# Four unused tiles in layer 1: split weights, quarter sums and the last projection's tiles begin at other addresses modulo 256 bytes

## The chip, the core and the metric

The kernel runs on one core of a Trainium2 chip. The metric is the device time of one execution in microseconds (us). Addresses in this text are byte addresses inside one partition of the on-chip memory, as the built program assigns them; "modulo 256" is what is left of them after division by 256.

## The reference

Two layers of a diffusion backbone over 1024 latent and 256 context tokens of width 1024, all in float32. Layer 0 has neighbourhood attention and bidirectional mLSTM heads; layer 1, which the change touches, has 16 bidirectional HGRN2 heads:

```python
def _c_mixer(h_lat, h_ctx, w_in, lb, h_norm, w_out, need_ctx):
    def project(h):
        q, f_fwd, f_bwd, i, z = _split_cols(h @ w_in, C_SIZES)     # 5 x 2048 columns, 16 heads of 128
        ...
        rec = (_bht(_heads(jax.nn.silu(q), HG_HEADS)), _bht(_heads(i, HG_HEADS)), (decay(f_fwd), decay(f_bwd)))
        return rec, z
    ...
    o_l, o_c = _gla_bidir(rec_l, rec_c, need_ctx)                  # chunked scan, both directions

    def merge(o, z):
        o = _rms(jnp.swapaxes(o, 1, 2).astype(z.dtype), h_norm.reshape(HG_HEADS, HG_VDIM))
        return (o.reshape(o.shape[:2] + (HG_VW,)) * jax.nn.silu(z)) @ w_out
    return merge(o_l, z_l), ...
...
x = x + gate * y_lat
```

## The kernel before, in words

Every large product is made of three float32r matmuls. Each operand is split into a high part (rounded to float32r by ScalarE, ACT) and a low part (the rest, subtracted by VectorE, DVE). `dense` (L129 to L133) walks over the 128-row blocks k and issues high x high (L131), high x low (L132) and low x high (L133) into one accumulator. In the profile a matmul is named `out<-moving,stationary`: `mm<-wzh,hh` streams the weight tile wzh past the stationary block of hh. TensorE (PE) loads the stationary block of the next matmul (PEld) while the present one streams.

The activations after norm and modulation lie in `hh` and `hl` (128 partitions x 8 blocks x 1280 tokens). Layer 1 then has three stages.

- **Wide stage** (1832 to 2165 us of the profiled span). `hg_wide` computes queries and forget gates with a Strassen-like scheme on quarters. `half_sums` makes three sums of quarters of the activations in tiles st1h to st3l (st4 is a fourth, elsewhere). Matmuls `x<-st1h,wh`, `mm<-hh,wh` and so on stream 512 columns of a sum or of hh past a weight block of the ring w.
- **Head stage** (2165 to 3141 us), 16 heads of about 62.5 us. `hg_vt` and `hg_vz` project values and z with the split weights wzh and wzl. For 256 context tokens hh streams past wz (`mm<-hh,wzh`); for the latent tokens wz streams past hh (`mm<-wzh,hh`, 256 columns), eight runs of 24 matmuls in each head. `hg_intra` puts such a run between the seven levels of the recurrence, whose small matmuls (L1401, `s<-gQ,gksel`) wait for DVE's updates of gK and gQ (L1431) and ACT's copy gksel (L1436). After the levels come the state products (`s<-gv,gkn`), the scan (`s<-gS,gQ`, `s<-gv,gA`) and ACT's squares of its results (L1506).
- **Last projection** (3141 to 3317 us), again with a Strassen-like scheme: `c<-woh,yh`, `tr<-woh,yh` stream 512 columns of a split weight past a split block of the head outputs. Weights come from rings in the pools oy, w1 and wo1, the y blocks from oy and op1.

Pools are stacked, so a tile's address follows from what was allocated ahead of it. The order of instructions is set by a scheduler that works with modelled times and with the waits that reused memory brings: hga, hgb and hg (head stage) lie where st and s1 (wide stage) lay, and a tile there waits for the old tiles that it overlaps.

Addresses modulo 256 before: hh and hl 192; wzh and wzl 0; st1h to st3l 0, st4h and st4l 192; the weight ring w of layer 1 192; in the last projection y blocks 192 (oy) and 64 (op1), weights 192 (oy, w1) and 64 (wo1). In layer 0 hh is at 192 too, and the ring w at 128. "Distance" below means address of the moving tile minus address of the stationary one, modulo 256. Offsets inside these tiles are multiples of 256 bytes.

Of the kernel before, what the change touches and what calls it, by code (L numbers as in the profile page):

```python
# [10 lines left out]
F32 = mybir.dt.float32  # L11
# [8 lines left out]
P = 128  # L20
# [25 lines left out]
class Prog:  # L46
# [489 lines left out]
    def ml_load(self, h, pool):  # L536
        nc = self.nc
        st = {"k": {}, "q": {}, "v": {}, "S": {}}

        def load(t0, order):  # L540
            q = self.rope("q", h, t0, pool, "mqT", 6)
            kT = self.rope("k", h, t0, pool, "mkT", 2)
            for i in order:
# [15 lines left out]
                for j in range(2):  # L559
                    nc.tensor.matmul(ps, lhsT=kT[:, j, s], rhs=q[:, j, s], start=(j == 0), stop=(j == 1))  # L560
                st["S"][tt] = self.t(pool, [P, P], F32, "mST", MLB)
                nc.scalar.copy(st["S"][tt], ps)

# [24 lines left out]
    def ml_rec(self, h, st, pool, nxt):  # L588
# [20 lines left out]
        for i in range(NT):  # L609
            for d in range(2):  # L610
# [8 lines left out]
                nc.vector.scalar_tensor_tensor(  # L619
                    out=SD, in0=st["S"][c], scalar=KS, in1=Dm, op0=ALU.mult, op1=ALU.mult  # L620
                )
# [408 lines left out]
    def half_sums(self, pool, s1, tp, x):  # L1030
        A, chain = self.half_part, self.half_chain
        home = {1: s1, 2: pool, 3: pool, 4: tp}
        two = lambda n: [self.t(home[n], [P, 4, 512], F32R, f"st{n}{c}", 1) for c in "hl"]
        S = {n: two(n) for n in (2, 3, 1)}
        self.p1 = lambda u: self.t(tp, [P, 512], F32, "p1", 3)
        self.co = lambda: self.t(tp, [P, 512], F32, "co", 2)
        add, sub = ALU.add, ALU.subtract

        def done(n, j, y):
            self.split(S[n][0][:, j, :], S[n][1][:, j, :], y)  # L1040

        yield two(4)
        S[4] = two(4)
        x = x + [self.half_base(self.t(tp, [P, 512], F32, f"u{j}", 1), j) for j in (2, 3)]
        for j in range(4):
            done(1, j, x[j])
        yield
        for j in (2, 3, 0, 1):
            (h, l), (h2, l2) = A(0, 0, j), A(1, 0, j)
            y = self.co()  # L1050
            chain(y, h, (l, add))
            chain(x[j], x[j], (y, sub))
            done(2, j, x[j])
            chain(y, y, (h2, sub), (l2, sub))
            done(3, j, y)
        for j in (2, 3, 0, 1):
            h, l = A(0, 1, j)
            chain(x[j], h, (x[j], sub), (l, add))
            done(4, j, x[j])
        yield S  # L1060
# [506 lines left out]
    def build(self):  # L1567
        tc, nc, a = self.tc, self.nc, self.a
        dma = nc.sync.dma_start
        with ExitStack() as es:  # L1570
# [280 lines left out]
            with l1:  # L1851
                lo = ExitStack()
                sp, s1 = [lo.enter_context(tc.tile_pool(name=n, bufs=1, reuse_waits="tile")) for n in ("st", "s1")]
                pools = []

                def early():
                    lo.close()
                    for n, tags in (
                        ("hga", (("gq", 2, 512), ("gK", 1, 2 * LAT), ("gQ", 1, 2 * LAT), ("gkn", 4, 512), ("gksel", 1, LAT))),
                        ("hgb", ()),  # L1860
                    ):
                        pools.append(l1.enter_context(tc.tile_pool(name=n, bufs=2, reuse_waits="tile")))
                        for t, b, f in tags:
                            for _ in range(b):
                                self.t(pools[-1], [P, f], F32, t, b)
                    pools.append(self.wblock(
                        pools[1], "wz", [a["wc"][:, i * 2048 : i * 2048 + P] for i in (3, 4)], KD, 256, [tp, 7, "br"]
                    ))
                    pools.append(self.hg_proj(0, pools[0], FF)[0])

                with tc.tile_pool(name="sx", bufs=1, side="right", reuse_waits="tile") as tp, self.pp.phase(x=4):
                    self.hg_wide(sp, s1, tp, x, FF[2][0], early)
                    wf = self.wblock(
                        self.wp, "w", [a["wc"][:, 4096 + P : 4096 + 2 * P]], KD, P, [tp, 7, "br"], ring=self.slabs
                    )
                pool, wzp, wv, st = pools
                pool = _Two(
                    pool, wzp, l1.enter_context(tc.tile_pool(name="hg", bufs=2, reuse_waits="tile")),
                    ("gq", "gK", "gQ", "gkn", "gksel"), ("wzl", "wzh"),
                )  # L1880
# [124 lines left out]
                for t in range(4):  # L2005
# [3 lines left out]
                        1, False, True,  # L2009
                    )  # L2010
            with tc.tile_pool(name="op1", bufs=2) as op, ExitStack() as wl, tc.issue_after(w5_dma.ins):
                wl1 = wl.enter_context(tc.tile_pool(name="wo1", bufs=1))
                r16 += [(wl1, "wo", 12)] * 8
                w6 = block(self.sw[2], r16, later)
# [254 lines left out]
```

## Time and profile before

| | |
|---|---|
| runs | 3320.68, 3319.92, 3318.21 us; median 3319.92 |
| profiled execution | 3318.67 us, span from first to last instruction 3316.9 us |
| granted TensorE clock | 1.00 |
| PE busy | 3268.9 us (99%) |
| PEld busy | 2905.1 us (88%) |
| DVE, ACT, POOL busy | 2173.8 (66%), 1455.9 (44%), 796.5 us (24%) |
| mean DMA rate | 115 GB/s |

"Busy" of PE is the union of the matmuls' modelled spans, which overlap: a 128x256 matmul is shown for some 280 ns, while the next one starts some 115 ns after it. How fast PE goes is therefore read from the spacing of starts, not from the share of busy time or from a matmul's own duration.

### The profile page before, as it was taken

To read this page: it belongs to the slowest core of one execution; us is meant where nothing else is said; L and a number is where in the kernel's file an instruction comes from. 1 tells how busy PE (TensorE), PEld (TensorE's weight loads), DVE (VectorE), ACT (ScalarE), POOL (GpSimd) and SP (SyncE) were. 2 spreads that over 40 slices of the span, in tenths; PEclk is the share of its full clock that TensorE was granted. 3 is DMA by queue.
4 is the path that set the end of the run, shared out by engine and by line. 5 is a ranking of instruction groups with operands and counts; after the bars stand their busy time and mean duration, and the time that the engine had idled before them with its cause. 6 is when DMAs were issued, how large, how long until landed. Compare 5 with 4: busy or idle time off the path is not lost.

```text
span 3316.9 us, 64819 instructions
## 1 busy us (share of the span) xinstructions
PE 3268.9 (99%) x24814; PEld 2905.1 (88%) x24814; DVE 2173.8 (66%) x4978; ACT 1455.9 (44%) x3396; POOL 796.5 (24%) x1191
## 2 busy tenths in 40 slices
PE   7999999999999999999999999999999999999999
PEld 6699899988989888898888788899999999999977
DVE  5337666666655566687767755577677677677756
ACT  5335554455544444455446333333433433433443
POOL 2222222222211112221110233312333333333110
PEclk9999999999999999999999999999999999999999
DMA  7713222232233433444653333322322324334376
GB/s 246 247 52 84 85 71 82 69 94 84 72 87 105 145 113 123 131 141 144 210 179 100 100 102 105 104 74 76 120 76 93 117 79 112 95 85 107 91 213 165
DMA packets 338102, 379.82 MB, mean 115 GB/s; under 512 B 34600, under 2 KB 269800, under 8 KB 336768
## 3 DMA queue, kind: packets, MB, share of 16 engines
q1 hardware_dynamic: 286032, 236.73, 24.2%
q0 software_dynamic: 51760, 138.94, 13.3%
q8 instruction: 196, 3.21, 0.4%
q14 instruction: 114, 0.93, 0.1%
HBM read 272.31 MB, written 103.08 MB: 113 GB/s over the span
## 4 chain that ended last, share of the span: by engine, by line
PE 80%; DVE 7%; issue 5%; DMA 4%; ACT 2%; POOL 1%; SPq 1%; DVEq 0%; POOLq 0%; ACTq 0%
PE mm L131 15%; PE mm L132 14%; PE mm L133 14%; PE acc L861 2%; PE s L1401 2%; PE tr L841 2%; PE mm L923 2%; PE mm L925 2%; PE mm L924 2%; PE x L131 2%; PE x L133 2%; PE x L132 2%; PE acc L633 2%; PE s L642 2%; PE s L1472 1%
## 5 line engine op out<-in xcount | busy, mean ns | idle before, releaser
L131 PE MATMUL mm<-wh,hh 128*128 128x256 f32 (+1 forms) x1440 | 446.2, 310 | 2.2 <-DVE graw L1694 0.8
L132 PE MATMUL mm<-wl,hh 128*128 128x256 f32 (+1 forms) x1440 | 444.9, 309 | 0.0
L133 PE MATMUL mm<-wh,hl 128*128 128x256 f32 (+1 forms) x1440 | 442.2, 307 | 0.0
L131 PE MATMUL mm<-hh,wh 128*128 128x512 f32 (+1 forms) x1076 | 392.0, 364 | 1.0 <-ACT p L1211 0.7
L132 PE MATMUL mm<-hl,wh 128*128 128x512 f32 (+1 forms) x1076 | 387.6, 360 | 0.7 <-DVE hl L318 0.7
L133 PE MATMUL mm<-hh,wl 128*128 128x512 f32 (+1 forms) x1076 | 387.4, 360 | 0.0
L131 PE MATMUL mm<-wzh,hh 128*128 128x256 f32 x1024 | 296.4, 289 | 0.0
L131 PEld LDWEIGHTS mm<-wh,hh 128*128 128x128 f32 x1440 | 271.6, 189 | 21.1 <-ACT ev L352 3.4
L132 PE MATMUL mm<-wzl,hh 128*128 128x256 f32 x1024 | 286.2, 280 | 0.0
L133 PE MATMUL mm<-wzh,hl 128*128 128x256 f32 x1024 | 285.6, 279 | 0.0
L132 PEld LDWEIGHTS mm<-wl,hh 128*128 128x128 f32 x1440 | 271.6, 189 | 12.3 <-issue 0.7
L133 PEld LDWEIGHTS mm<-wh,hl 128*128 128x128 f32 x1440 | 271.4, 189 | 12.0 <-issue 0.5
L131 PEld LDWEIGHTS mm<-hh,wh 128*128 128x128 f32 x1076 | 202.9, 189 | 33.5 <-ACT ev L371 4.2
L133 PEld LDWEIGHTS mm<-hh,wl 128*128 128x128 f32 x1076 | 202.6, 188 | 29.7 <-issue 0.2
L132 PEld LDWEIGHTS mm<-hl,wh 128*128 128x128 f32 x1076 | 202.9, 189 | 28.6 <-DVE hl L318 1.4
L131 PEld LDWEIGHTS mm<-wzh,hh 128*128 128x128 f32 x1024 | 192.8, 188 | 2.4
L132 PEld LDWEIGHTS mm<-wzl,hh 128*128 128x128 f32 x1024 | 192.7, 188 | 0.0
L133 PEld LDWEIGHTS mm<-wzh,hl 128*128 128x128 f32 x1024 | 192.0, 188 | 0.0
L74 DVE TENSOR_TENSOR wl<-wraw,wh 128x512 fp32r<-128x512 f32 x174 | 118.6, 689 | 85.6 <-ACT wh L73 83.8
L1436 ACT COPY gksel<-gK 128x1024 f32<-128x1024 f32 x96 | 110.9, 1155 | 100.1 <-DVE gK L1431 43.7
L1431 DVE TENSOR_TENSOR gQ<-gQ,gF 128x1024 f32<-128x1024 f32 x112 | 140.4, 1253 | 20.4 <-PE s L1401 20.4
L1431 DVE TENSOR_TENSOR gK<-gK,gF 128x1024 f32<-128x1024 f32 x112 | 140.2, 1251 | 18.8 <-ACT gksel L1436 11.4
(598 smaller groups left out, 8523.8 us busy)
## 6 DMA issues: line engine op xcount, KB each, us to landing
wraw<-in_wab_dram SPq DMA_DIRECT2D x108, 256.0 KB
wraw<-yd SPq DMA_DIRECT2D x92, 256.0 KB
br<-in_wc_dram SPq DMA_DIRECT2D x66, 256.0 KB
md<-ev POOLq DMA_DIRECT2D x60, 256.0 KB, 2.6
wraw<-in_wc_dram SPq DMA_DIRECT2D x120, 128.0 KB
mloz<-md SPq DMA_DIRECT2D x40, 256.0 KB
s<-gyt POOLq DMA_DIRECT2D x36, 256.0 KB, 5.7
adar<-in_wada_dram SPq DMA_DIRECT2D x16, 512.0 KB
```

The lines of the kernel that those rows point to most:

```text
L74: nc.vector.tensor_tensor(out=lo, in0=x, in1=hi.bitcast(F32), op=ALU.subtract)
L131: mm(ps, lhsT=lh(k), rhs=rh(k), start=(start and k == 0), stop=False, skip_group_check=skip)
L132: mm(ps, lhsT=lh(k), rhs=rl(k), start=False, stop=False, skip_group_check=skip)
L133: m = mm(ps, lhsT=ll(k), rhs=rh(k), start=False, stop=(stop and k == nk - 1), skip_group_check=skip)
L633: nc.tensor.matmul(num, lhsT=qc[:, j, :], rhs=C[d][:, j, :], start=False, stop=(j == 1))
L642: nc.tensor.matmul(u, lhsT=st["k"][c][:, j * P : (j + 1) * P], rhs=vw, start=True, stop=True)
L841: nc.tensor.transpose(pt[:nk, i, :], pr[:, o : o + nk], self.ident)
L861: m = nc.tensor.matmul(yp[h64], lhsT=v[:, h64], rhs=pTs[hd][:nk, i, :], start=(i == turn[0]), stop=(i == turn[-1]), tile_position=(0, hd * ...
L923: mm(ps, lhsT=yh[k], rhs=w.h(kk), start=(kk == 0), stop=False)
L924: mm(ps, lhsT=yh[k], rhs=w.l(kk), start=False, stop=False)
L1431: nc.vector.tensor_tensor(out=v, in0=v, in1=tot, op=ALU.mult)
L1436: m = nc.scalar.copy(ksel.rearrange("p (b s i) -> p b s i", s=2, i=h), pick(K))
```

## The change

Four tiles are allocated that nothing writes or reads; they only move what is allocated behind them. No computing instruction is added or removed.

```diff
@@ half_sums @@
         two = lambda n: [self.t(home[n], [P, 4, 512], F32R, f"st{n}{c}", 1) for c in "hl"]
+        self.t(pool, [P, 48], F32, "pad", 1)
         S = {n: two(n) for n in (2, 3, 1)}
+        self.t(s1, [P, 48], F32, "pad", 1)
@@ build, early @@
                                 self.t(pools[-1], [P, f], F32, t, b)
+                    self.t(pools[1], [P, 96], F32, "pad", 1)
                     pools.append(self.wblock(
                         pools[1], "wz", [a["wc"][:, i * 2048 : i * 2048 + P] for i in (3, 4)], KD, 256, [tp, 7, "br"]
                     ))
@@ build, last projection @@
             with tc.tile_pool(name="op1", bufs=2) as op, ExitStack() as wl, tc.issue_after(w5_dma.ins):
+                self.t(op, [P, 32], F32, "pad", 1)
                 wl1 = wl.enter_context(tc.tile_pool(name="wo1", bufs=1))
```

What moves, as the two builds place it:

| tiles | modulo 256 before | after | matmuls and their distance before, after |
|---|---|---|---|
| wzh, wzl | 0 | 128 | 3,072 that stream wz past hh, hl: 64, 192 |
| | | | 384 that stream hh, hl past wz: 192, 64 |
| st1h to st3l | 0 | 192 | 576 that stream them past the ring w: 64, 0 |
| weights in wo1, y blocks in op1 | 64 | 192 | 203 that stream wo1's weights past oy's y blocks: 128, 0; the rest of the last projection keeps its distance |
| head-stage tiles of the pool hg (gv, gz, gS, gA, gD, gF of odd heads, wraw, gyt) | 0 | 128 | 256 `s<-gS,gQ` and 224 `s<-gv,gkn`: 0, 128 |

Since wzl now overlaps st1l too, the scheduler puts a few instructions of the first head elsewhere. On DVE, ahead of the first head, the four subtractions that make wzl (each piece of wzh must be there) stood ahead of p and of three more splits of the wide stage:

```order
L74 TENSOR_TENSOR wl_24605<-br_24492,wh_24604 128x512
L74 TENSOR_TENSOR wzl_24715<-br_24717,wzh_24716 128x512
L74 TENSOR_TENSOR wzl_24715<-br_24722,wzh_24716 128x512
L74 TENSOR_TENSOR wzl_24715<-br_24727,wzh_24716 128x512
L74 TENSOR_TENSOR wzl_24715<-br_24732,wzh_24716 128x512
L1066 TENSOR_TENSOR p_5056_24603<-x_24602,p_5049_24567 128x512
L74 TENSOR_TENSOR wl_24622<-br_24333,wh_24621 128x512
```

Now they stand eleven instructions later on DVE, between the first head's own preparations gkn and gQ:

```order
L74 TENSOR_TENSOR wzl_24718<-br_24720,wzh_24719 128x512
L74 TENSOR_TENSOR wzl_24718<-br_24725,wzh_24719 128x512
L1367 TENSOR_TENSOR gkn_24885<-gK_24881 128x512
L1367 TENSOR_TENSOR gkn_24884<-gK_24881 128x512
L74 TENSOR_TENSOR wzl_24718<-br_24730,wzh_24719 128x512
L1370 TENSOR_TENSOR gQ_24883<-gq_24742,gF_20438 128x512 x2
L74 TENSOR_TENSOR wzl_24718<-br_24735,wzh_24719 128x512
L1370 TENSOR_TENSOR gQ_24883<-gq_24744,gF_20438 128x512 x2
L74 TENSOR_TENSOR wl_24803<-br_24805,wh_24804 128x512
```

So gQ, and what follows it on DVE, stands behind four instructions that it did not stand behind before; ACT's casts to wzh move back in the same way, behind six others. On PE, in the first head, the two transposes of gEc stood behind a level's matmuls (L1401) and three of wz:

```order
L133 MATMUL mm_24934<-wzh_24716,hl_20308 128x256
L1401 MATMUL s_24959<-gQ_24880,gksel_24960 64x64 x16
L131 MATMUL mm_24934<-wzh_24716,hh_20307 128x256
L132 MATMUL mm_24934<-wzl_24715,hh_20307 128x256
L133 MATMUL mm_24934<-wzh_24716,hl_20308 128x256
L1293 MATMUL tr_24874<-ident_82,gEc_24872 128x128 x2
L131 MATMUL mm_24934<-wzh_24716,hh_20307 128x256
```

Now they stand inside the run of wz matmuls ahead of that level:

```order
L131 MATMUL mm_24937<-wzh_24719,hh_20307 128x256
L132 MATMUL mm_24937<-wzl_24718,hh_20307 128x256
L1295 MATMUL tr_24877<-ident_82,gEc_24875 128x128 x2
L133 MATMUL mm_24937<-wzh_24719,hl_20308 128x256
L131 MATMUL mm_24937<-wzh_24719,hh_20307 128x256
```

That is a move by eleven rows on PE, in the first head alone. In the other 15 heads, on SP, POOL and everywhere else the order is the same, but for line numbers.

## The prediction

> **What bounds the kernel now.** I read the page's busy times first, then the waits of PE in the head stage, then the timeline of PE, run by run.
>
> ```profile
> span 3316.9 us, 64819 instructions
> PE 3268.9 (99%) x24814; PEld 2905.1 (88%) x24814; DVE 2173.8 (66%) x4978; ACT 1455.9 (44%) x3396; POOL 796.5 (24%) x1191
> ...
> PE 80%; DVE 7%; issue 5%; DMA 4%; ACT 2%; POOL 1%; SPq 1%; DVEq 0%; POOLq 0%; ACTq 0%
> ```
>
> PE is never idle for long, and 80% of the chain that ended last is matmuls. Nothing in the change removes one, so the only thing that can move the time by much is the spacing at which PE starts matmuls of one and the same shape. Does that spacing differ, and along with what? The next fence has four stretches of 128x256 matmuls, each by its first and last row; in a stretch every start follows the one before it, three lines in turn.
>
> ```profile
> 188.51 0.28 PE L133 MATMUL mm<-wh,hl 128*128 128x256 f32 x1
> ...
> 193.60 0.28 PE L133 MATMUL mm<-wh,hl 128*128 128x256 f32 x1
> ...
> 230.86 0.28 PE L131 MATMUL mm<-wh,hh 128*128 128x256 f32 x1
> ...
> 236.39 0.28 PE L133 MATMUL mm<-wh,hl 128*128 128x256 f32 x1
> ...
> 2727.53 0.28 PE L132 MATMUL mm<-hl,wzh 128*128 128x256 f32 x1
> ...
> 2730.03 0.28 PE L133 MATMUL mm<-hh,wzl 128*128 128x256 f32 x1
> ...
> 2737.53 0.28 PE L132 MATMUL mm<-wzl,hh 128*128 128x256 f32 x1
> ...
> 2740.12 0.28 PE L133 MATMUL mm<-wzh,hl 128*128 128x256 f32 x1
> ```
>
> The first stretch has 45 steps in 5.09 us, 113.1 ns each; the second 47 in 5.53 us, 117.7; the third 22 in 2.50 us, 113.6; the fourth 22 in 2.59 us, 117.7. By the addresses of the built program the first three lie at distance 192 and the fourth, the wz matmuls that the change is about, at 64. Distance 192 shows two speeds, near 113.5 and near 117.7, and distance 64 mostly the slower one. The granted clock is 1.00 throughout, so this is no throttle.
>
> [...]
>
> How often is distance 192 fast? Layer 0 has 35 unbroken runs of at least 22 steps at that distance, the first and the last of which begin at
>
> ```profile
> 183.05 0.28 PE L132 MATMUL mm<-wl,hh 128*128 128x256 f32 x1
> ...
> 1182.00 0.37 PE L131 MATMUL mm<-wh,hh 128*128 128x256 f32 x1
> ```
>
> Twenty-seven of them average near 113.8 ns and eight 117.8; together 0.77 x 113.8 + 0.23 x 117.8 = 114.7. Several of the fast ones begin with some five slow steps and drop then; none climbs back.
>
> For 512 columns the order of the distances is another one:
>
> ```profile
> 2143.59 0.40 PE L131 MATMUL x<-st1h,wh 128*128 128x512 f32 x1
> ...
> 2146.35 0.40 PE L131 MATMUL x<-st2h,wh 128*128 128x512 f32 x1
> ...
> 2149.10 0.28 PE L131 MATMUL tr<-hh,wh 128*128 128x256 f32 x1
> ...
> 2154.71 0.40 PE L131 MATMUL x<-st3h,wh 128*128 128x512 f32 x1
> ...
> 2157.51 0.40 PE L131 MATMUL mm<-hh,wh 128*128 128x512 f32 x1
> ...
> 2160.27 0.39 PE L131 MATMUL x<-hh,wh 128*128 128x512 f32 x1
> ...
> 2162.99 0.39 PE L131 MATMUL x<-st4h,wh 128*128 128x512 f32 x1
> ...
> 2165.71 0.28 PE L131 MATMUL mm<-hh,wzh 128*128 128x256 f32 x1
> ...
> 3262.31 0.39 PE L131 MATMUL c<-woh,yh 128*128 128x512 f32 x1
> ...
> 3265.10 0.39 PE L131 MATMUL tr<-woh,yh 128*128 128x512 f32 x1
> ```
>
> Twelve matmuls stand between the rows of each pair. st1, st2 and st3 (distance 64) take 2.76, 2.75 and 2.80 us: 230.8 ns a step. hh, hh and st4 (distance 0) take 2.76, 2.72 and 2.72 us: 227.8. The last pair (distance 128) takes 2.79 us: 232.5.
>
> **The change, part by part.**
>
> *wz past hh (3,072 matmuls, 64 to 192).* Not all of a gain would reach the end, since DVE holds PE back once in every head:
>
> ```profile
> PE s L1401 <- DVE gQ L1431: 8.0, 15, 0.5
> ...
> 2739.57 1.22 DVE L1431 TENSOR_TENSOR gQ<-gQ,gF 128x1024 f32<-128x1024 f32 x1
> ...
> 2740.93 1.15 PE L1401 MATMUL s<-gQ,gksel 128*64 128x64 f32 x32 [0.54 <-DVE gQ L1431]
> ...
> 2743.58 1.22 DVE L1431 TENSOR_TENSOR gQ<-gQ,gF 128x1024 f32<-128x1024 f32 x1
> ...
> 2745.43 1.15 PE L1401 MATMUL s<-gQ,gksel 128*64 128x64 f32 x32
> ```
>
> PE waits 0.54 us at the third level. The two wz runs ahead of it lie in DVE's shadow: what they gain or lose changes that wait alone. One level on, gQ ends at 2744.80 and PE starts 0.63 us after that, where the waiting start came 0.14 us after its release: 0.49 us of room, and a faster run needs 24 x 3 ns = 0.07. So the six later runs count in full: 6 x 23 steps x 16 heads = 2,208 steps, from 117.7 to 114.7 ns, **-6.6 us**. Bounds: no run turns fast, 0; all do, 2,208 x 4.4 = -9.7.
>
> *hh past wz (384 matmuls, 192 to 64).* From 113.6 to 117.7 ns, 24 x 4.1 = 0.10 us in each head, ahead of the same wait, which shrinks from 0.54 to 0.44: **0**. Without that cover it would be +1.6 in 16 heads.
>
> *st1 to st3 (576 matmuls, 64 to 0).* PE alone sets the pace there; 576 x (230.8 - 227.8) = **-1.7 us**, between 0 and -2.4 (at the quickest pair's 226.7).
>
> *Last projection (203 matmuls, 128 to 0).* 203 x (232.5 - 227.8) = **-1.0 us**, between 0 and -1.2. PE sets the pace there too, and the final stores follow on its last matmuls.
>
> *Small float32 matmuls (`s<-gS,gQ`, `s<-gv,gkn`, 0 to 128).* No row has them at 128. The nearest are the 480 matmuls above, of the same engine, two passes each: if they moved like a 256-column step between its extremes, 4.6 ns x 960 = 4.4 us either way. Nothing in the trace gives the sign, and 512 columns rank the distances in another order than 256 do, so I take **0**, the middle, and keep 1 us of it for the range.
>
> *First head.* DVE's four wzl subtractions move behind what they preceded:
>
> ```profile
> 2147.72 2.64 DVE L74 TENSOR_TENSOR wzl<-br,wzh 128x512 fp32r<-128x512 f32 x4
> ...
> 2168.89 0.69 DVE L1176 TENSOR_TENSOR co<-co,u 128x512 f32<-128x512 f32 x1 [0.40 <-ACT co L1174]
> ...
> 2170.61 0.69 DVE L1176 TENSOR_TENSOR co<-co,p 128x512 f32<-128x512 f32 x1 [0.69 <-ACT co L1174]
> 2171.22 1.22 DVE L1431 TENSOR_TENSOR gQ<-gQ,gF 128x1024 f32<-128x1024 f32 x1
> ...
> 2174.08 1.22 PE L1401 MATMUL s<-gQ,gksel 128*64 128x64 f32 x32
> ```
>
> gQ (ends 2172.44) comes 2.64 us later, less the idle 0.40 and 0.69, so it ends at 2173.99; gD now ahead of it adds 0.6: 2174.6. PE wanted it at 2174.08, so it waits about **+0.6 us**, once; 0 to +2.6. Queued behind the subtractions are gkn and gQ of the first head, and for them PE's first small matmuls.
>
> Sum: -6.6 - 1.7 - 1.0 + 0.6 = -8.7 us. Against the profiled execution's 3318.67 that is 3310.0; the median of the runs is 1.25 us above it, so **3311.2 us**, 0.26% faster. The four pads themselves cost nothing: no instruction touches them.
>
> **Rivals.**
>
> *No change (3318).* The spacing is set by what PE did just before a run, not by the distance. For it: within one head, at the same distance 64, the run behind two transposes steps at 113.2 ns (22 steps in 2.49 us) where the others take 117.7:
>
> ```profile
> 2733.06 0.28 PE L132 MATMUL mm<-wzl,hh 128*128 128x256 f32 x1
> ...
> 2735.55 0.28 PE L133 MATMUL mm<-wzh,hl 128*128 128x256 f32 x1
> ```
>
> Then the six later runs stay slow, and -1.7 - 1.0 + 0.6 = -2.1 us is left, 3317.8, and with half of the 512-column terms 3319.2. Against it: the slow start of many runs at 192 drops after five steps, which none at 64 does. [...]
>
> *Slower: the stores of gyt (3349).* gyt begins at 128 instead of 0. If its stores took longer, ACT's next write of gyt, which waits for them, would hold gksel back, and with it PE:
>
> ```profile
> 2745.52 0.69 ACT L1555 ACTIVATE gyt<-tr,hnc 128x512 f32<-128x512 f32 x1 [1.05 <-DMA s<-gyt]
> 2747.17 1.06 ACT L1436 COPY gksel<-gK 128x1024 f32<-128x1024 f32 x1 [0.96 <-PE tr L1332]
> ...
> s<-gyt POOLq DMA_DIRECT2D x36, 256.0 KB, 5.7
> ...
> fd<-co POOLq DMA_DIRECT2D x32, 256.0 KB, 2.5
> ...
> yd<-gyt POOLq DMA_DIRECT2D x30, 256.0 KB, 2.6
> ```
>
> ACT has 0.96 us of room there, so it decides from 0.96 us more on. At twice the 5.7 us that such a store takes in the head stage, up to 5.7 - 0.96 = 4.7 us in each of the 8 heads with a shifted gyt would be lost, +38 us, and 3311.2 would become 3349. Against it: co lies at 192 and its stores take 2.5 us, those of gyt at 0 in the other stage take 2.6. [...]
>
> **How the numbers follow.** The distance decides: 0.73, with 3306.5 to 3316 as its own range (all terms at their good ends, -9.7 - 2.4 - 1.2 - 1.0 + 0.6 = -13.7, and three of the six runs slow). The run's beginning decides: 0.22. The stores: 0.05. Less than 0.2% (6.6 us) can hardly be told from no change here; of the first case 0.62 lies beyond that and 0.11 within it. So faster 0.62, same 0.33, slower 0.05, and 3306.5 to 3319 holds the time 8 times in 10.
>
> **What would show it.** In the changed kernel's timeline: wz runs of the later levels at 113 to 114 ns a step, `mm<-hh,wzh` at 117.7, a wait at the third level of some 0.5 us still, head periods about 0.4 us shorter; st1 to st3 at 228, `c<-woh,yh` at 227 everywhere; one wait of PE near 2174 us. I am wrong if the wz runs stay at 117.7, or if they turn fast while PE's waits on gQ grow by as much.

## The result, and the profile after

The changed kernel takes 3313.05 us (median of 12 runs, 3309.35 to 3315.65) against 3320.57 us (12 runs, 3317.82 to 3322.05): ratio 0.9978, 95% interval 0.9969 to 0.9987. That is 7.5 us less, between 4 and 10 by the interval. Forecast were 3311.2 us and 0.26%.

The profiled execution after has this span and these busy times:

```profile
span 3312.1 us, 64823 instructions
PE 3261.9 (98%) x24814; PEld 2900.8 (88%) x24814; DVE 2173.9 (66%) x4978; ACT 1456.7 (44%) x3396; POOL 794.5 (24%) x1191
```

Its span is only 4.8 us shorter, so this one execution shows less of the gain than the medians do. It was already 0.5 us behind the profile before at 1820 us, where nothing is changed. It lost 0.8 us between 1832 and 1900 us: the granted clock is at 0.50 for 3.4 us from 1850.7 us on, which it is not in the profile before, though PE's pause of 1.98 us ahead of it is the same in both. And 1.9 us went in one late head, told below.

PE's timeline after, at the same place as the slow wz run of before (2737.53 to 2740.12 there), and at the run behind the transposes of gq in the same head:

```profile
2736.35 0.28 PE L132 MATMUL mm<-wzl,hh 128*128 128x256 f32 x1
...
2738.84 0.28 PE L133 MATMUL mm<-wzh,hl 128*128 128x256 f32 x1
2739.69 1.15 PE L1403 MATMUL s<-gQ,gksel 128*64 128x64 f32 x32 [0.57 <-DVE gQ L1433]
...
2745.17 0.66 PE L1334 MATMUL tr<-ident,gq 128*128 128x128 f32 x4
...
2745.79 0.28 PE L132 MATMUL mm<-wzl,hh 128*128 128x256 f32 x1
...
2748.38 0.28 PE L133 MATMUL mm<-wzh,hl 128*128 128x256 f32 x1
```

The first run's 22 steps take 2.49 us, 113.2 ns, where before they took 2.59. PE's wait on gQ behind it is still there. The run behind gq did not gain: 22 steps in 2.59 us, 117.7 ns. So it is over the 16 heads: behind gA 113.8 ns on the mean, behind gv and gknc 113.6, behind gQ and gK 113.7, behind gq 117.8; before, all four were at 117.8. (A place is named by the small matmuls or transposes that stand just ahead of the run.)

The first small matmuls of two heads that follow each other, before and then after (columns: shortest, median and longest ns, then when the group ran), from the answers on that line:

```profile
L1401 PE MATMUL s<-gq,gkn x32: 221/222/271, 2667.7 to 2668.7; 128*64 128x64 f32 x32
L1401 PE MATMUL s<-gq,gkn x32: 221/222/269, 2730.2 to 2731.2; 128*64 128x64 f32 x32
```

```profile
L1403 PE MATMUL s<-gq,gkn x32: 222/222/270, 2667.0 to 2667.9; 128*64 128x64 f32 x32
L1403 PE MATMUL s<-gq,gkn x32: 222/222/270, 2729.0 to 2730.0; 128*64 128x64 f32 x32
```

A head takes 62.0 us instead of 62.5; over most heads 62.04 against 62.50.

At 512 columns, the wide stage and the last projection after:

```profile
2143.34 0.39 PE L131 MATMUL x<-st1h,wh 128*128 128x512 f32 x1
...
2146.06 0.39 PE L131 MATMUL x<-st2h,wh 128*128 128x512 f32 x1
...
3255.83 0.39 PE L131 MATMUL c<-woh,yh 128*128 128x512 f32 x1
...
3258.55 0.39 PE L131 MATMUL c<-woh,yh 128*128 128x512 f32 x1
```

Twelve steps of st1 now take 2.72 us, 226.7 ns (before 2.76), and of the last projection 2.72 (before 2.79 at distance 128).

One thing became slower, the first head. PE's waits after, then its granted clock in four stretches there (columns: stretch, length, busy time and count of PE, PEld, DVE, ACT and POOL, clock, share and rate of DMA), then the subtraction that PE waited for:

```profile
PE s L1403 <- DVE gQ L1433: 8.3, 15, 0.7
PE s L1403 <- DVE p L1068: 2.3, 1, 2.3
```

```profile
2170.50:2171.50 1.00, 0.93 (x31) 0.93 (x33) 0.57 (x2) 0.81 (x2) 0.00 (x0) 1.00 0.01 0
2171.50:2173.40 1.90, 1.90 (x40) 1.79 (x36) 1.76 (x4) 0.49 (x2) 1.08 (x2) 0.51 0.29 44
2173.40:2175.00 1.60, 1.60 (x9) 1.59 (x8) 1.47 (x2) 1.18 (x1) 0.00 (x0) 0.51 1.00 311
2175.00:2177.00 2.00, 2.00 (x19) 2.00 (x18) 1.90 (x3) 0.37 (x1) 0.00 (x0) 1.00 0.80 203
```

```profile
2169.84 0.68 DVE L1068 TENSOR_TENSOR p<-x,p 128x512 f32<-128x512 f32 x1
```

Before, this p began at 2167.81 us, ahead of PE's need. Now it stands behind the moved wzl subtractions, PE idles 2.3 us, and from 1 us after the pause the clock is at half for 3.4 us.

### The profile page after: what moved, and what is told of

It is laid out like the page before. It is cut to its first block, busy times and chain, and to the rows that moved or that the text cites. A ratio compares the mean times of both kernels' runs of the same rounds, so it can differ in the third digit from the quotient of the medians.

```text
span 3312.1 us, 64823 instructions
## 1 busy us (share of the span) xinstructions
PE 3261.9 (98%) x24814; PEld 2900.8 (88%) x24814; DVE 2173.9 (66%) x4978; ACT 1456.7 (44%) x3396; POOL 794.5 (24%) x1191
## 4 chain that ended last, share of the span: by engine, by line
PE 87%; DVE 4%; DMA 3%; issue 3%; ACT 2%; POOL 1%; SPq 1%; DVEq 0%; POOLq 0%; ACTq 0%
PE mm L131 16%; PE mm L132 15%; PE mm L133 15%; PE s L1403 4%; PE acc L861 2%; PE mm L923 2%; PE mm L925 2%; PE mm L924 2%; PE tr L841 2%; PE x L131 2%; PE x L132 2%; PE x L133 2%; PE acc L633 2%; PE s L642 2%; PE s L1474 1%
## 5 line engine op out<-in xcount | busy, mean ns | idle before, releaser
L1433 DVE TENSOR_TENSOR gK<-gK,gF 128x1024 f32<-128x1024 f32 x112 | 139.1, 1242 | 18.2 <-ACT gksel L1438 11.4
```

Source lines behind the costliest of these rows:

```text
L1433: nc.vector.tensor_tensor(out=v, in0=v, in1=tot, op=ALU.mult)
```

## The experiments

Each timed kernel is set against runs of the kernel before that were made beside it.

**One pad at a time.** The pad ahead of wz alone; the order of the instructions is that of before:

```diff
+                    self.t(pools[1], [P, 96], F32, "pad", 1)
                     pools.append(self.wblock(pools[1], "wz", ...
```

> Only the pad of 384 bytes ahead of wzh and wzl (wz from 0 to 128, distance of its matmuls to hh from 64 to 192, hg pool from 0 to 128); the order of instructions is that of before. If the distance sets the spacing: wz runs at 113.6 ns behind all small matmuls but the gq transposes, as in the changed kernel, head period 62.04 us instead of 62.50, no wait of 2.3 us at the first head; 16 x 0.46 = 7.4 us less than before, 3313 us against 3320.5. If the gain came from the order at the first head or from the other pads: wz runs at 117.7, 3320 us.

Measured 3312.5 us against 3319.59, ratio 0.998 (0.9971 to 0.9989): -7.1 us. Head period 62.04 us, the wz runs as in the changed kernel, and no wait for p. This pad brings nearly all of the gain. The pads around st1 to st3 alone:

```diff
+        self.t(pool, [P, 48], F32, "pad", 1)
         S = {n: two(n) for n in (2, 3, 1)}
+        self.t(s1, [P, 48], F32, "pad", 1)
```

> Only the two pads of 192 bytes around st1h to st3l (distance of their 576 matmuls to the ring from 64 to 0); wz stays at 64. This pad alone brings the other order at the first head. If distance and order both count: wide stage 2.1 us shorter, first head 2.9 us longer (PE waits some 2.3 us for p at about 2170 us and the granted clock falls to 0.5 for some 3 us), heads at 62.50; together +0.8 us, 3321 us. If the wait in the changed kernel was chance: -2.1 us, 3318.4. If the distance does nothing: +2.9 us, 3323.4.

Measured 3320.37 us against 3319.59, ratio 1.0002 (0.9993 to 1.001). Its waits and its clock at the first head:

```profile
PE s L1403 <- DVE p L1068: 2.3, 1, 2.3
```

```profile
2172.50:2174.50 2.00, 2.00 (x44) 2.00 (x42) 1.87 (x4) 0.83 (x2) 0.95 (x2) 0.50 0.14 37
2174.50:2176.00 1.50, 1.50 (x20) 1.38 (x18) 0.85 (x2) 0.57 (x1) 0.12 (x1) 0.61 0.93 253
```

The same wait and the same slow clock, though wz is where it was: the order that the st pads bring makes the wait, and in both profiles that have it the slow clock follows. Between 2164 and 2240 us this kernel falls 3.2 us behind the kernel before. The 576 matmuls step at 227.0 ns instead of 229.8, -1.6 us, and 312 matmuls `mm<-hh,wh` among them, whose distance was 0 all along, at 227.2 instead of 229.4, -0.7 us: loss and gain cancel within 1 us. The pad in op1 alone:

```diff
+                self.t(op, [P, 32], F32, "pad", 1)
                 wl1 = wl.enter_context(tc.tile_pool(name="wo1", bufs=1))
```

> Only the pad of 128 bytes in op1 (203 matmuls of the last projection from distance 128 to 0), order as before. If the prediction's size was right, 203 x 4.7 ns: -1.0 us, 3319.5. If what the changed kernel's profile shows for the last stage is due to this pad: -2.2 us, 3318.3. If distance does nothing there: 3320.5.

Measured 3318.37 us against 3319.59, ratio 0.9996 (0.9987 to 1.0005), which alone does not tell -1.0 from nothing or from -2.2. The spacing tells that the matmuls did get faster: the 203 go from 232.6 to 226.7 ns, -1.2 us. The three differences add to -7.1 + 0.8 - 1.2 = -7.5 us, that of the whole change; as each is known to some 3 us only, that they fit so closely is luck.

**All pads without the other order.** A pad of 192 bytes at the head of hga as well, so that the head stage's tiles overlap the same old tiles as before. Since it moves wz too, the pad ahead of wz shrinks from 384 to 192 bytes, and wz stays at 128:

```diff
+                        if n == "hga":
+                            self.t(pools[-1], [P, 48], F32, "pad", 1)
                         for t, b, f in tags:
...
-                    self.t(pools[1], [P, 96], F32, "pad", 1)
+                    self.t(pools[1], [P, 48], F32, "pad", 1)
```

> All pads of the changed kernel and one more of 192 bytes at the head of hga, so that hga's tiles overlap the same tiles of st as before; the order of instructions at the first head is then that of before, and gq, gK, gQ, gkn and gksel begin at 192 instead of 0. If the order at the first head costs the changed kernel its wait and the slow clock behind it: no such wait, 2.9 us less than the changed kernel, -7.4 - 2.1 - 2.2 = -11.7 us, 3309 us. If the wait comes from the shared memory and not from the order: as the changed kernel, 3313 us. If the addresses of hga's tiles matter for the small matmuls, head periods differ from 62.04 us.

Measured 3308.16 us against 3319.59, ratio 0.9963 (0.9951 to 0.9976): -11.4 us, faster than both kernels. No wait for p at the first head. Here gq, gK, gQ, gkn and gksel begin at 192, and the run behind its transposes, at the same distance 192 as in the changed kernel, is fast:

```profile
2740.50 0.65 PE L1334 MATMUL tr<-ident,gq 128*128 128x128 f32 x4
...
2741.11 0.28 PE L132 MATMUL mm<-wzl,hh 128*128 128x256 f32 x1
...
2743.62 0.28 PE L133 MATMUL mm<-wzh,hl 128*128 128x256 f32 x1
```

22 steps in 2.51 us; 113.9 ns over all heads against 117.8. That takes the head period to 61.94 us. With its pad alone wz had the order of before and that run stayed slow in 15 of 16 heads, so the order isn't what frees it. What moved are the tiles of the transposes of gq and of the small matmuls ahead of them, not the run; which of the two decides was not separated.

**Other distances for wz.** The same one pad in three other sizes, `[P, 48]`, `[P, 16]` and `[P, 64]`:

> Only a pad of 192 bytes ahead of wzh and wzl: wz begins at 192 like hh, distance 0 both ways; order as before. If the distance decides: the 256-column rows of the kernel before at distance 0 step at 119.9 ns, so 2,208 steps of the six later runs take 2.1 ns more each, head period 62.8 us, +4.7 us, 3324 us. If what matters is only that wz no longer begins at 0 (its own address, not the distance): 113.6 ns, head period 62.04, 3313 us.

> Only a pad of 64 bytes ahead of wzh and wzl: wz begins at 64, distance 128 both ways, which no 256-column run of the kernel before has. If distances rank at 256 columns as at 512 (0 best, 192 worst), they would not have come out as they did; so no forecast from rows but bounds: between 113.5 and 119.9 ns, head period 62.0 to 62.8 us, 3313 to 3324 us. If wz's own address matters and 0 is the bad one: 62.04 us and 3313 us.

> Only a pad of 256 bytes ahead of wzh and wzl: all tiles behind it move by 256 bytes, so nothing changes modulo 256; order as before. If addresses modulo 256 decide: as before, wz runs at 117.7 ns, head period 62.50, 3320 us. If it is the place in memory (another stretch of it, other neighbours): as the pad of 384 bytes, 62.04 us and 3312.5 us.

| kernel | wz at | distance | wz runs, ns | head period, us | us | ratio |
|---|---|---|---|---|---|---|
| before | 0 | 64 | 117.8 | 62.50 | | |
| pad of 192 | 192 | 0 | 119.3 to 119.9 | 62.77 | 3323.33 against 3319.91 | 1.0011 (1.0002 to 1.002) |
| pad of 64 | 64 | 128 | 118.4 to 119.5 | 62.64 | 3322.55 | 1.0006 (0.9997 to 1.0016) |
| pad of 256 | 0 | 64 | 117.8 | 62.50 | 3319.92 | 1.0 (0.9991 to 1.0009) |
| pad of 384 | 128 | 192 | 113.5 to 114.1, one at 117.6 | 62.04 | 3312.5 against 3319.59 | 0.998 (0.9971 to 0.9989) |

A move by 256 bytes does nothing, one by 192 makes the kernel slightly slower: neither the place in memory nor "not at 0" decides, but the address modulo 256. A head of the pads of 192 and of 256:

```profile
L1401 PE MATMUL s<-gq,gkn x32: 222/222/270, 2671.4 to 2672.3; 128*64 128x64 f32 x32
L1401 PE MATMUL s<-gq,gkn x32: 222/222/270, 2734.1 to 2735.0; 128*64 128x64 f32 x32
```

```profile
L1401 PE MATMUL s<-gq,gkn x32: 222/222/270, 2668.9 to 2669.8; 128*64 128x64 f32 x32
L1401 PE MATMUL s<-gq,gkn x32: 222/222/270, 2731.4 to 2732.3; 128*64 128x64 f32 x32
```

62.7 and 62.5 us.

**The spacing by itself.** A kernel that computes nothing of the reference but runs of 48 such matmuls, one after the other, with one small copy for each run:

```python
for i in range(16):
    p.run("n" + LET[i], 256, 16 * i)      # 256 columns, moving tile 16*i bytes past the stationary one
for i in range(16):
    p.run("w" + LET[i], 512, 16 * i)
...
```

> No model: runs of 48 float32r matmuls by themselves, in the three-line pattern, with nothing beside them but one small copy for each run; na to np: 256 columns, moving tile 0 to 240 bytes behind the stationary one modulo 256 in steps of 16; wa to wp: 512 columns; s..: 256 columns with stationary tiles at other addresses; f, g, h, i: 256 columns behind 2 transposes-like float32 matmuls, 8 of them, 32 narrow ones, and 32 narrow and 2; za to zm: float32 128 columns. If the distance decides: about 119.9 ns at distance 0, 117.7 or 113.5 at 64, 113.5 at 192, the same at every address of the stationary tile; at 512 columns 227, 229.5, 232.5, 234 at 0, 64, 128, 192. If the run's start decides: the four distances alike within one kind of start, and different between starts. If other engines' traffic is what spaces the matmuls: all alike here.

The starts of runs in its timeline (ne: distance 64, nh: 112, ni: 128, nm: 192; wa: 0, we: 64; fm: 192 behind two float32 matmuls; ze: 64 and zi: 128, float32):

```profile
59.29 0.28 PE L60 MATMUL ne<-mh,sh 128*128 128x256 f32 x1
...
64.94 0.28 PE L60 MATMUL nf<-mh,sh 128*128 128x256 f32 x1
...
76.46 0.28 PE L60 MATMUL nh<-mh,sh 128*128 128x256 f32 x1
...
81.90 0.28 PE L60 MATMUL ni<-mh,sh 128*128 128x256 f32 x1
...
87.59 0.28 PE L60 MATMUL nj<-mh,sh 128*128 128x256 f32 x1
...
104.63 0.28 PE L60 MATMUL nm<-mh,sh 128*128 128x256 f32 x1
...
110.09 0.28 PE L60 MATMUL nn<-mh,sh 128*128 128x256 f32 x1
...
392.02 0.28 PE L61 MATMUL fm<-ml,sh 128*128 128x256 f32 x1
...
396.97 0.28 PE L61 MATMUL fm<-ml,sh 128*128 128x256 f32 x1
...
512.33 0.28 PE L69 MATMUL ze<-fp 128*128 128x128 f32 x1
...
517.69 0.28 PE L69 MATMUL zi<-fp 128*128 128x128 f32 x1
...
523.05 0.28 PE L69 MATMUL zm<-fp 128*128 128x128 f32 x1
```

48 steps take 5.65 us at 64 (117.7 ns), 5.44 at 112 (113.3), 5.69 at 128 (118.5) and 5.46 at 192 (113.8, of which the last 20 are at 113.3). At 0 a step takes 120.0 ns. The other distances lie between, at 116.7 to 120.0 in their last 20 steps. With the stationary tile at 0, 64, 128 or 192 the last 20 steps were the same to 0.1 ns at each of the four distances: the difference of the addresses counts, not the addresses. But fm, also at 192, takes 42 steps in 4.95 us, 117.9 ns, and stays there, and so does gm, behind eight float32 matmuls. Behind 32 narrow ones (hm), or 32 narrow ones and two wide (im), a run at 192 comes down to 113.3. So at such a distance there is more than one pace, and what stands ahead of a run picks it. At 512 columns the last 20 steps are at 226.7, 228.8, 232.6 and 233.3 ns at 0, 64, 128 and 192, as in the whole kernel. Beside them ran only the small copy for each run, so traffic of other engines isn't needed for it. The float32 runs, 24 matmuls of two records each, take 5.36 us at 64 and at 128 alike, 111.7 ns a record.

**Distance 112 in the kernel.** The probe had 112 at 113.3 ns from the first step on, so wz was put there, on top of the kernel without the other order. wzh and wzl become one tile that is used from its 112th byte on, and the pad ahead of wz goes; the tiles of hg come to 64 by it:

```diff
+                both = self.t(pool, [P, 4128], F32R, "wzh", 1)
+                whole = [both[:, i : i + 2048].rearrange("p (a b) -> p a b", b=512) for i in (28, 2076)]
```

> The kernel without the reorder (e4), with wzl and wzh in one tile that is read and written from its 112th byte on, so that wz begins at 48 and its 3,072 matmuls lie at distance 112 from hh (the 384 the other way at 144) instead of 192; order as before. In the probe distance 112 stepped at 113.3 ns from the first step on, where 192 lost some 25 ns at a run's start or stayed at 117.8 behind some starts. If that carries over: all seven wz runs at 113.4, head period 61.9 us, about 1 us less than e4, 3307 us. If a run's start in the kernel can hold it in a slow pace here too: up to 118.7 to 120, head period 62.6 to 62.8, 3319 us. If more bits than the distance modulo 256 count (the probe had the distances 16 to 240 only with a stationary tile at 128): anything between.

Measured 3310.59 us against 3320.02, ratio 0.9975 (0.9966 to 0.9984): faster than before by 9.4 us, but not than distance 192. The forecast from the probe missed. A run behind the transposes of gA:

```profile
2731.82 0.28 PE L136 MATMUL mm<-wzh,hh 128*128 128x256 f32 x1
...
2732.64 0.28 PE L137 MATMUL mm<-wzh,hl 128*128 128x256 f32 x1
...
2734.34 0.28 PE L137 MATMUL mm<-wzh,hl 128*128 128x256 f32 x1
```

The first 7 steps take 0.82 us, 117 ns, the next 15 take 1.70, 113.3. Nearly all wz runs here (107 of 112) have five to nine slow steps at their start, then 113.3; at 192, without the other order, most have one to four. The head period is 62.15 us against 61.94. In the probe the run at 112 followed another run without a gap; in the kernel the runs stand behind small matmuls. The probe has no run at 112 behind small matmuls.

## Why the prediction was right, and where it was off

**wz past hh: -6.6 forecast, -7.1 measured** with its pad alone. The working held: the time came from spacing, the runs ahead of the third level's wait counted for nothing, and the six later runs in full. The sizing assumed that 23% of the steps stay slow, from a count in layer 0 (layer 0 has ten slow runs beside the 27 fast ones, not eight; that is 27%, by which the term is about -6). In fact it is not a share of runs at random but one run of six, that behind gq, in every head. With 113.7 ns in five runs and 117.8 in the sixth, the mean is 114.4 instead of 114.7. That a share from layer 0 lay near one in six was luck.

**hh past wz: 0 forecast, 0 found.** `mm<-hh,wzh` and its companions step at 117.8 ns now (113.8 before), and PE's waits on gQ are 8.3 us in 15 heads (8.0 before): the shadow still holds. The room of 0.49 us at the next level was enough.

**st1 to st3: -1.7 forecast, -1.7 found, and 0.7 more** that was not: the `mm<-hh,wh` runs between them became faster too, with no change of their distance. Whether the pace carries over from the run ahead (226.9 ns at st1 to st3, 227.2 here) no run tests by itself. By all steps st1 to st3 were at 229.8 ns and are at 226.9: the prediction's rows had both a nanosecond too high, which cancels. From 1900 to 2164 us, where no slow clock disturbs it, the changed kernel gains 1.8 us on the one before.

**Last projection: -1.0 forecast, -1.2 by the spacing** (203 steps from 232.6 to 226.7 ns), **and 0.3 more** at the matmuls whose distance was 0 all along (422 steps before, from 227.9 to 227.1).

**Small float32 matmuls: 0 forecast and 0 found.** `s<-gS,gQ` steps at 111.7 ns before and 111.6 after, `s<-gv,gkn` at 111.6 and 111.5, and the probe has no dependence either.

**First head: +0.6 forecast, +3.2 found**, beyond the prediction's own bound of +2.6. This step failed. Between 2164 and 2240 us the changed kernel loses 2.7 us on the one before, in a stretch where the kernel with the wz pad alone gains 0.4. The prediction followed the delay of 2.6 us to gQ and to the second of PE's levels, and allowed for DVE's idle time ahead of it. It overlooked that p, the last subtraction of the wide stage, stands behind the same four instructions, with no idle time in between, and that the head's very first small matmuls wait for it. And the pause of 2.3 us had a second price that was not in the sum: 3.4 us at half clock. That is up to 1.7 us of work; of it some 0.9 us was left at 2240 us (3.2 less the pause's 2.3), since PE's wait for ACT's gksel in that head, 0.4 us before, is gone. Both profiles with this pause show the half clock behind it; whether it comes in every execution isn't known.

**The sum.** -7.1 - 1.7 - 0.7 - 1.2 - 0.3 + 3.2 = -7.8, against -7.5 measured (4 to 10 by the interval) and -8.7 forecast. The forecast came out near because a part that was not foreseen made up for some of the first head.

**The rivals.** "No change" fell in the table above, but its mechanism did not: what precedes a run matters beside the distance, as gq shows (at distance 192, 117.8 ns behind gq, 113.7 behind the others). Gyt's stores took 5.3 us (5.7 before), so nothing was late there.

**A late head, left open.** In one late head PE lost 1.6 us in the profile after, waiting for gkn, which stood on ACT behind a cast whose weights were late. SP's queue of loads had waited for a store of weight sums; its wait before, after, and in the pad of 256, and that pad's small matmuls:

```profile
SPq L104 <- DMA sw<-wraw: 7.5, 1, 7.5
```

```profile
SPq L104 <- DMA sw<-wraw: 11.2, 1, 11.2
```

```profile
SPq L104 <- DMA sw<-wraw: 10.6, 1, 10.6
```

```profile
2967.47 3.45 PE L1472 MATMUL s<-gv,gkn 128*128 128x128 f32 x20 [1.83 <-ACT gkn L1414]
```

Since the pad of 256 has the pace of before and the same wait, the pace isn't its cause. But it is not shown to come by itself: in all seven profiles of kernels whose wz and hg tiles moved, that head takes longer than its neighbours (by 0.3 to 3.7 us), and in none of the three others (before, the pads of st and of op1 alone) by more than 0.2. With one profile for each kernel, whether the moved tiles bring it stays open; the kernel with the pad of 256 has the same median as the one before.

Left open: what in PE or in the memory sets these paces. The runs show that it is the difference of the addresses (120.0 ns at 0, 113.3 at 112) and the start of a run (at 192, 113.8 ns in nm, 117.9 in fm), not how.

## What to carry to other kernels

When PE is busy all the time, compare the spacing of starts of equal matmuls in different stages; if it differs at full clock, look at the addresses of the moving and the stationary tile modulo 256 before looking elsewhere. Try a pad, but measure it in place, since here the best distance depended on the width (at 512 columns 226.7 ns at 0 and 233.3 at 192, at 256 columns 120.0 and 113.3) and the pace also on what ran just ahead (at 192, 113.8 ns in nm and 117.9 in fm). And check what a moved tile does to the order of instructions: follow each delayed instruction to everything behind it in its queue, the releases of buffers first.

## What the hardware showed that was not expected

- float32r matmuls of 256 columns start 113.3 to 120.0 ns apart by the distance of their operands modulo 256 bytes; at 512 columns 226.7 to 234.7. The order of the distances isn't the same at the two widths, and not monotone (at 256 columns 120.0 at 96, 113.3 at 112, 118.7 at 128).
- At one distance two paces are possible: 113.3 or 117.8 ns at 64 and at 192, 118.7 or 120.0 at 128. A run may hold the slower one to its end.
- The float32 matmuls, each of which leaves two records in the trace, were indifferent to it: 111.7 ns a record at 0, 64, 128 and 192.
- The length of a pause alone does not decide whether the granted clock falls to 0.50 (for 3.4 us each time). All ten profiles of the whole kernel have PE's pause of 1.98 us in the wide stage; the clock fell within 2 us behind it in three of them and not in seven. It fell after pauses of 2.29 (the changed kernel and the st pads alone), 2.20 (the changed kernel), 1.83 (pad of 256) and 1.82 us (pad of 192), and stayed at 1.00 after 2.39, 2.09, 1.86 (distance 112), 1.70 and 1.61 us (the changed kernel).
